# A hybrid Mamba-2 / Conformer step on one core: the chunk-state product of the scan as three float32r passes on split operands, instead of one plain float32 product

## The chip, the cores and the metric

The program runs on 1 core of one Trainium2 chip. The metric is the device time of one execution in microseconds (us), as the median of the timed runs.

## What is computed

Two decoder layers run over a prompt of 2048 tokens (width 1024) and 8 single-token samples. Layer 0 is a Mamba-2 SSD mixer, layer 1 a gated Conformer convolution. Inputs and outputs are float32. The change lies in the chunked scan of layer 0, over the prompt: 32 heads of 64 channels in 4 groups, state size 128, 16 chunks of 128 tokens. The reference, cut to that part:

```python
def ssd_scan(x, dt, A, Bm, Cm, h0, chunk):
    ...
    a_cum = jnp.cumsum(dts * A.reshape(G, R), axis=2)
    xdt = xs * dts[..., None]
    ...
    cb = jnp.einsum('bcqgn,bckgn->bcqkg', Cs, Bs)
    y_diag = jnp.einsum('bcqkg,bcqkgr,bckgrp->bcqgrp', cb, decay, xdt)
    states = jnp.einsum('bcqgn,bcqgr,bcqgrp->bcgrpn', Bs, jnp.exp(a_cum[:, :, -1:] - a_cum), xdt)
    chunk_decay = jnp.exp(a_cum[:, :, -1])
    def step(h, inp):
        dec, st = inp
        return dec[..., None, None] * h + st, h
    h_fin, prev = lax.scan(step, h_init, (chunk_decay, states))
    y_off = jnp.einsum('bcqgn,bcgrpn,bcqgr->bcqgrp', Cs, prev, jnp.exp(a_cum))
    y = y_diag + y_off
```

`states` is the product that the change touches: for one group and one chunk, B transposed (tokens x state, 128 x 128) against the weighted inputs of the group's 8 heads (128 tokens x 512 channels).

## The kernel before, in words

The large projections of the kernel (`mm_in`, line 163, and `out_mm`, line 709) are already made in three float32r passes: each operand is split into a rounded high part and the rest, and hi x hi, lo x hi and hi x lo are summed in PSUM. The small products of the scan are plain float32 matmuls.

The order of the work is written out by hand: each engine runs its instructions strictly in the order in which the code issues them, and tiles of a pool are given out in turn, so that a new tile waits until the last readers of the tile whose memory it takes are done. `bufs` is the number of such places.

The scan is a loop over 64 **units** `u`, one for each pair of group and chunk (16 chunks of a group one after the other). It is software-pipelined by one unit and woven with the projection of the gate z:

- `ssd_loads(u + 2)` brings xg (inputs), bcg (B and C) and rb (decay sums, one buffer) by DMA from the SP queue.
- `ssd_a(u + 1)` prepares a unit: the decay matrix E (eight heads, half started on ACT at L579, half on DVE at L581, exponentials on ACT at L589 and L591), eA on ACT (L586, L587), transposes of xg on TensorE into ps_tx (L595), the transpose of B and the product B x C into ps_b (L597, L598), then on DVE xdt (L601) and Xd (L602) out of ps_tx, bt on ACT (L604) out of ps_b, cbm on DVE (L606) and E times cbm on DVE (L609).
- `zstep` issues some steps of the z projection: 8 matmuls each, three steps for a z tile of 264, 256, 512, 512 and 512 columns in turn, 3 or 4 steps for a unit. Its results are copied out by ACT (zt, L525); the weights are split by ACT (wh, L98) and POOL (wl, L99).
- `ssd_b(u)` finishes a unit: eight heads' products on TensorE into ps_d (L621), the chunk's state product into ps_st (L623), the product with the carried state into ps_o (L636); then on DVE yt (L626, four times), yt's second part (L637), the state update (L638, L639) and the sum (L640), and a DMA of yt to DRAM issued by POOL (L641).

All PSUM tiles of the scan have one buffer. Xd, bt, yt, E, eA and xdt have two.

Of the kernel before, what the change touches and what calls it, by code (L numbers as in the profile page):

```python
# [7 lines left out]
F32 = mybir.dt.float32  # L8
F32R = mybir.dt.float32r
AF = mybir.ActivationFunctionType  # L10
ALU = mybir.AluOpType
# [4 lines left out]
P = 128  # L16
# [22 lines left out]
def hybrid_step(ctx: ExitStack, tc: tile.TileContext, I, O):  # L39
    nc = tc.nc  # L40
    V, A, G_, TE, SY = nc.vector, nc.scalar, nc.gpsimd, nc.tensor, nc.sync
# [476 lines left out]
    sd = Pool("ssd", 2)  # L518
# [24 lines left out]
    def zstep(n):  # L543
        for _ in range(n):
            next(zg, None)
# [7 lines left out]
    ld, stA, state = {}, {}, {}  # L553

    def ssd_loads(u):
        if u >= len(units):
            return
        g, c = units[u]
        j, cc = divmod(c, 4)
        xg = sd.tile([P, 4, P], "xg", bufs=3)  # L560
        SY.dma_start(xg, x_d[j][cc, :, 4 * g:4 * g + 4, :])
        bcg = sd.tile([P, 2, P], "bcg", bufs=3)
        SY.dma_start(bcg, bc_d[j][cc, :, g, :, :])
        rb = sd.tile([P, 8, P], "rb", bufs=1)
        SY.dma_start(rb, ac_d[c:c + 1, 8 * g:8 * g + 8, :].to_broadcast([P, 8, P]))
        ld[u] = (xg, bcg, rb)

    def ssd_a(u):
        if u >= len(units):
            return  # L570
        g, c = units[u]
        j, cc = divmod(c, 4)
        xg, bcg, rb = ld[u]
        hs = slice(8 * g, 8 * g + 8)
        E = sd.tile([P, 8, P], "E")
        for h in range(8):
            ah = acT[:, cc, j, 8 * g + h:8 * g + h + 1]
            if h < EA_:
                A.activation(E[:, h, :], rb[:, h, :], AF.Relu, bias=ah, scale=-1.0)  # L579
            else:  # L580
                V.tensor_scalar(E[:, h, :], rb[:, h, :], ah, 0.0, ALU.subtract, ALU.min)  # L581
        eA = None
        if c:
            eA = sd.tile([P, 4, P], "eA")
            rv = rb.rearrange("p (a two) t -> p a two t", two=2)
            A.activation(eA[0:64], rv[0:64, :, 0, :], AF.Exp)  # L586
            A.activation(eA[64:128], rv[64:128, :, 1, :], AF.Exp)  # L587
        if EA_:
            A.activation(E[:, :EA_], E[:, :EA_], AF.Exp, scale=-1.0)  # L589
        if EA_ < 8:  # L590
            A.activation(E[:, EA_:], E[:, EA_:], AF.Exp)  # L591
        px = pss.tile([P, 8, 64], "ps_tx")
        pxf = px.rearrange("p a b -> p (a b)")
        for i in range(4):
            TE.transpose(pxf[:, i * P:(i + 1) * P], xg[:, i, :], ident)  # L595
        pb = pss.tile([P, 2, P], "ps_b")
        TE.transpose(pb[:, 0, :], bcg[:, 0, :], ident)  # L597
        TE.matmul(pb[:, 1, :], bcg[:, 0, :], bcg[:, 1, :], start=True, stop=True)  # L598
        xdt = sd.tile([P, 8, 64], "xdt")
        Xd = sd.tile([P, 8, 64], "Xd")  # L600
        V.tensor_tensor(xdt, px, dtT[:, cc, j, hs].unsqueeze(2).to_broadcast([P, 8, 64]), ALU.mult)  # L601
        V.tensor_tensor(Xd, px, wtT[:, cc, j, hs].unsqueeze(2).to_broadcast([P, 8, 64]), ALU.mult)  # L602
        bt = sd.tile([P, P], "bt")
        A.activation(bt, pb[:, 0, :], AF.Copy)  # L604
        cbm = sd.tile([P, 1, P], "cbm", bufs=1)
        V.tensor_tensor(cbm[:, 0, :], pb[:, 1, :], tri, ALU.mult)  # L606
        if EM:
            G_.tensor_tensor(E[:, :EM], E[:, :EM], cbm.to_broadcast([P, EM, P]), ALU.mult)
        V.tensor_tensor(E[:, EM:], E[:, EM:], cbm.to_broadcast([P, 8 - EM, P]), ALU.mult)  # L609
        stA[u] = (E, eA, xdt, Xd, bt)  # L610

    def ssd_b(u):
        g, c = units[u]
        j, cc = divmod(c, 4)
        xg, bcg, rb = ld.pop(u)
        E, eA, xdt, Xd, bt = stA.pop(u)
        hs = slice(8 * g, 8 * g + 8)
        pd = pss.tile([P, 4, P], "ps_d")
        for h in range(8):
            o = 64 * (h % 2)  # L620
            TE.matmul(pd[o:o + 64, h // 2, :], xdt[:, h, :], E[:, h, :], start=True, stop=True)  # L621
        pst = pss.tile([P, 8, 64], "ps_st")
        TE.matmul(pst.rearrange("p a b -> p (a b)"), bt, Xd.rearrange("p a b -> p (a b)"), start=True, stop=True)  # L623
        yt = sd.tile([P, 4, P], "yt")
        for i in range(4):
            V.scalar_tensor_tensor(yt[:, i, :], xg[:, i, :], Dch[:, 4 * g + i:4 * g + i + 1], pd[:, i, :], ALU.mult, ALU.add)  # L626
        if c == 0:
            stt = sd.tile([P, 8, 64], "state", bufs=1)
            state[g] = stt
            V.tensor_copy(stt, pst)  # L630
        else:
            stt = state[g]
            po = pss.tile([P, 4, P], "ps_o")
            sf = stt.rearrange("p a b -> p (a b)")
            for i in range(4):
                TE.matmul(po[:, i, :], sf[:, i * P:(i + 1) * P], bcg[:, 1, :], start=True, stop=True)  # L636
            V.tensor_tensor(eA, po, eA, ALU.mult)  # L637
            (G_ if SP_ else V).tensor_tensor(stt, stt, dec[:, cc, j, hs].unsqueeze(2).to_broadcast([P, 8, 64]), ALU.mult)  # L638
            V.tensor_tensor(stt, pst, stt, ALU.add)  # L639
            V.tensor_tensor(yt, yt, eA, ALU.add)  # L640
        G_.dma_start(y_d[c][:, 4 * g:4 * g + 4, :], yt)  # L641
        if c == NC - 1:
            G_.dma_start(O["ssm_p"][:, g, :], stt.rearrange("p a b -> p (a b)"))
# [3 lines left out]
    ZLEAD = 9  # L647
    zstep(ZLEAD)
    ssd_a(0)
    done = ZLEAD  # L650
    for u in range(len(units)):
        ssd_a(u + 1)
        ssd_loads(u + 2)
        want = ZLEAD + (ZN - ZLEAD) * (u + 1) // len(units)
        zstep(want - done)
        done = want
        ssd_b(u)
# [298 lines left out]
    for i in range(NCH):  # L956
        hl, _, nt, _ = fr[i]
# [423 lines left out]
    for i in range(NCH):  # L1381
        hl, nt = fr.pop(i)[:2]
# [109 lines left out]
```

## Time and profile before

| | |
|---|---|
| median of 3 timed runs | 3116.99 us (3115.62 to 3121.19) |
| the profiled execution | 3112.42 us, span 3110.6 us |
| busy share of the span: TensorE (PE) / DVE / ACT / POOL | 97% / 76% / 50% / 43% |
| the scan's first and last state product (L623) | 622.7 us and 1164.2 us after the span's start |

PE is TensorE's matrix product and PEld its weight load, DVE is VectorE, ACT is ScalarE, POOL is GpSimd, SP is the engine that issues most DMAs. In the list of instruction groups, a row has line, engine, operation, output<-inputs, shapes and count, then the busy time in us and the mean of one in ns, and after the second bar the engine's idle time just ahead of them with what ended it. In the timeline, a row has start and duration in us, engine, line, operation and count; neighbouring instructions of one kind are one row, and a bracket gives the idle time ahead and its releaser. A busy PE is not PE at its peak, since matmuls overlap and their ends are modelled; so the distance between starts is used for what a group of matmuls takes. A plain float32 matmul of the code leaves two records on PE.

### The profile page before, as it was taken

To read this page: it belongs to the slowest core of one execution; us is meant where nothing else is said; L and a number is where in the kernel's file an instruction comes from. 1 tells how busy PE (TensorE), PEld (TensorE's weight loads), DVE (VectorE), ACT (ScalarE), POOL (GpSimd) and SP (SyncE) were. 2 spreads that over 40 slices of the span, in tenths; PEclk is the share of its full clock that TensorE was granted. 3 is DMA by queue.
4 is the path that set the end of the run, shared out by engine and by line. 5 is a ranking of instruction groups with operands and counts; after the bars stand their busy time and mean duration, and the time that the engine had idled before them with its cause. 6 is when DMAs were issued, how large, how long until landed. Compare 5 with 4: busy or idle time off the path is not lost. (4 is left out here: it accounts for less than half of the span.)

```text
span 3110.6 us, 43242 instructions
## 1 busy us (share of the span) xinstructions
PE 3016.1 (97%) x16379; PEld 2540.5 (82%) x16379; DVE 2354.4 (76%) x3200; ACT 1540.4 (50%) x2601; POOL 1325.5 (43%) x983
## 2 busy tenths in 40 slices
PE   7999999999999999999989999999999999899998
PEld 6788888878878787788878888888888888677776
DVE  6556777678888884555448999999999997667663
ACT  6444434445555544444445555555545544655553
POOL 2112333211111111323325777867867767355551
PEclk9999999999999999999999999999999999999999
DMA  4123444455555556444451221111112124533331
GB/s 153 59 81 128 133 132 134 136 169 184 170 186 173 187 157 222 159 154 163 163 174 43 60 68 52 58 54 52 58 61 62 49 68 150 179 125 125 133 128 56
DMA packets 258624, 373.12 MB, mean 120 GB/s; under 512 B 30136, under 2 KB 187032, under 8 KB 252272
## 3 DMA queue, kind: packets, MB, share of 16 engines
q1 hardware_dynamic: 129168, 280.62, 28.0%
q10 hardware_dynamic: 122656, 67.68, 7.3%
q0 software_dynamic: 6592, 22.05, 1.8%
q8 instruction: 129, 2.11, 0.3%
q14 instruction: 79, 0.65, 0.1%
HBM read 240.47 MB, written 129.82 MB: 119 GB/s over the span
## 5 line engine op out<-in xcount | busy, mean ns | idle before, releaser
L1041 DVE SCALAR_TENSOR_TENSOR ps_acc<-vt,cw,ps_acc 128x1024 f32<-128x1024 f32 x672 | 815.1, 1283 | 6.5 <-ACT ps_acc L1034 4.8
L1047 POOL TENSOR_TENSOR pacc<-pacc,pr 128x1024 f32<-128x1024 f32 x256 | 620.7, 2457 | 110.4 <-ACT pr L1046 107.7
L709 PE MATMUL ps_out<-wo_hi,hhi 128*128 128x512 f32 (+1 forms) x1088 | 433.9, 399 | 9.0 <-ACT hhi L714 9.0
L709 PE MATMUL ps_out<-wo_lo,hhi 128*128 128x512 f32 (+1 forms) x1088 | 426.9, 392 | 0.0
L163 PE MATMUL ps_h<-u_hi,wh 128*128 128x512 f32 (+2 forms) x1920 | 397.2, 349 | 14.6 <-ACT zt L1082 8.0
L709 PE MATMUL ps_out<-wo_hi,hlo 128*128 128x512 f32 x1024 | 401.7, 392 | 0.8 <-DVE hlo L720 0.8
L163 PE MATMUL ps_h<-u_lo,wh 128*128 128x512 f32 (+2 forms) x1920 | 393.0, 347 | 0.0
L163 PE MATMUL ps_h<-u_hi,wl 128*128 128x512 f32 (+2 forms) x1920 | 392.7, 347 | 0.3 <-POOL wl L99 0.3
L163 PEld LDWEIGHTS ps_h<-u_hi,wh 128*128 128x128 f32 x1920 | 316.4, 190 | 62.6 <-ACT zt L1082 9.1
L163 PEld LDWEIGHTS ps_h<-u_lo,wh 128*128 128x128 f32 x1920 | 315.8, 189 | 45.1
L163 PEld LDWEIGHTS ps_h<-u_hi,wl 128*128 128x128 f32 x1920 | 315.3, 189 | 45.4 <-POOL wl L99 0.5
L295 DVE SCALAR_TENSOR_TENSOR acc<-raw,cw,acc 128x512 f32<-128x512 f32 (+1 forms) x360 | 229.1, 645 | 131.8 <-ACT acc L287 71.7
L1046 ACT ACTIVATE pr<-vt,cw 128x1024 f32<-128x1024 f32 x256 | 287.9, 1147 | 72.9 <-POOL pacc L1047 53.5
L99 POOL TENSOR_TENSOR wl<-wraw,wh 128x1024 fp32r<-128x1024 f32 x86 | 214.2, 2491 | 192.2 <-ACT wh L98 189.3
L709 PEld LDWEIGHTS ps_out<-wo_hi,hhi 128*128 128x128 f32 (+1 forms) x1088 | 201.5, 185 | 55.1 <-ACT hhi L714 9.8
L709 PEld LDWEIGHTS ps_out<-wo_lo,hhi 128*128 128x128 f32 (+1 forms) x1088 | 201.1, 185 | 48.5
L709 PEld LDWEIGHTS ps_out<-wo_hi,hlo 128*128 128x128 f32 x1024 | 193.9, 189 | 39.4 <-DVE hlo L720 1.6
L641 POOL DMA_DIRECT2D y_d<-yt x64 | 38.8, 606 | 437.3 <-DVE yt L640 414.3
L163 PE MATMUL ps_mm<-u_hi,wh 128*128 128x512 f32 (+2 forms) x960 | 200.2, 351 | 3.4 <-ACT wh L98 3.4
L163 PE MATMUL ps_mm<-u_lo,wh 128*128 128x512 f32 (+2 forms) x960 | 197.7, 349 | 0.0
L163 PE MATMUL ps_mm<-u_hi,wl 128*128 128x512 f32 (+2 forms) x960 | 197.4, 348 | 0.0
L163 PEld LDWEIGHTS ps_mm<-u_hi,wh 128*128 128x128 f32 x960 | 158.9, 191 | 27.1 <-ACT wh L98 3.9
(308 smaller groups left out, 4892.1 us busy)
## 6 DMA issues: line engine op xcount, KB each, us to landing
rb<-ac_d SPq DMA_DIRECT2D x64, 512.0 KB, 4.3
z_d<-zt ACTq DMA_DIRECT2D x96, 256.0 KB, 2.9
wraw<-w_in SPq DMA_DIRECT2D x48, 512.0 KB, 3.3
xg<-x_d SPq DMA_DIRECT2D x64, 256.0 KB, 3.3
y_d<-yt POOLq DMA_DIRECT2D x64, 256.0 KB, 2.8
wraw_o<-w_out SPq DMA_DIRECT2D x32, 512.0 KB, 4.1
yl<-y_d SPq DMA_DIRECT2D x16, 1024.0 KB, 6.2
zl<-z_d SPq DMA_DIRECT2D x16, 1024.0 KB, 5.5
```

The lines of the kernel that those rows point to most:

```text
L99: (eng or G_).tensor_tensor(wl, raw, wh.bitcast(F32), ALU.subtract)
L163: TE.matmul(ps[:, :n], a[:, k, :], x[:, k, o:o + n], start=(j == 0 and k == 0), stop=(j == 2 and k == KD - 1))
L295: V.scalar_tensor_tensor(acc[:, :n], raw[:, k:k + n], cw[:, m, k:k + 1], acc[:, :n], ALU.mult, ALU.add)
L641: G_.dma_start(y_d[c][:, 4 * g:4 * g + 4, :], yt)
L709: TE.matmul(pos[nh][:m], a[q][:, r, :m], w[q][:, r, ns], start=(k == 0 and j == 0), stop=(k == MI - 1 and j == len(parts) - 1))
L1041: V.scalar_tensor_tensor(acc, vt[:, k:k + W], cw1[:, m, k:k + 1], acc, ALU.mult, ALU.add)
L1046: A.activation(pr, vt[:, kk:kk + W], AF.Copy, scale=cw1[:, m, kk:kk + 1])
L1047: G_.tensor_tensor(pacc, pacc, pr, ALU.add)
```

## The change

bt is kept as two float32r tiles, bth (rounded copy, ACT as before) and btl (the rest, a new DVE subtraction out of ps_b, L605). A new step `ssd_split(u)` splits Xd into Xdh (a copy on ACT, L619) and Xdl (a subtraction on POOL, L620); it is called in the loop ahead of `ssd_a(u + 1)`. The state product becomes three float32r matmuls that add up in ps_st: Xdh x bth, Xdh x btl, Xdl x bth (L636). Xd and yt go from two buffers to one; Xdh and Xdl have one each. Line numbers behind that place move: L606 is L607, L609 is L610, L621 is L632, L623 is L636, L626 is L639, L636 to L641 are L649 to L654.

```diff
-        Xd = sd.tile([P, 8, 64], "Xd")
+        Xd = sd.tile([P, 8, 64], "Xd", bufs=1)
...
-        bt = sd.tile([P, P], "bt")
-        A.activation(bt, pb[:, 0, :], AF.Copy)
+        bt = [sd.tile([P, P], f"bt{i}", F32R) for i in "hl"]
+        A.activation(bt[0], pb[:, 0, :], AF.Copy)
+        V.tensor_tensor(bt[1], pb[:, 0, :], bt[0].bitcast(F32), ALU.subtract)
...
+    xsp = {}
+
+    def ssd_split(u):
+
+        Xd = stA[u][3].rearrange("p a b -> p (a b)")
+        xsp[u] = [sd.tile([P, 512], f"Xd{i}", F32R, bufs=1) for i in "hl"]
+        A.activation(xsp[u][0], Xd, AF.Copy)
+        G_.tensor_tensor(xsp[u][1], Xd, xsp[u][0].bitcast(F32), ALU.subtract)
+
     def ssd_b(u):
...
+        Xs = xsp.pop(u)
...
         pst = pss.tile([P, 8, 64], "ps_st")
-        TE.matmul(pst.rearrange("p a b -> p (a b)"), bt, Xd.rearrange("p a b -> p (a b)"), start=True, stop=True)
-        yt = sd.tile([P, 4, P], "yt")
+        pstf = pst.rearrange("p a b -> p (a b)")
+        for i, (w_, x_) in enumerate(((bt[0], Xs[0]), (bt[1], Xs[0]), (bt[0], Xs[1]))):
+            TE.matmul(pstf, w_, x_, start=i == 0, stop=i == 2)
+        yt = sd.tile([P, 4, P], "yt", bufs=1)
...
     for u in range(len(units)):
+        ssd_split(u)
         ssd_a(u + 1)
```

DVE in the middle of the scan, one unit's `ssd_a` and the start of `ssd_b`; what stands in brackets is what the instruction waits for. Before:

```order
L601 TENSOR_TENSOR xdt<-ps_tx,dtT 128x512 [waits PE_49]
L602 TENSOR_TENSOR Xd<-ps_tx,wtT 128x512
L606 TENSOR_TENSOR cbm<-ps_b,tri 128x128 [waits Activation_49]
L609 TENSOR_TENSOR E<-E,cbm 128x1024 [waits DVE_49]
L626 SCALAR_TENSOR_TENSOR yt<-xg,Dch,ps_d 128x128 [waits DMAHW3_49,DMASW2_49,PE_49]
```

The same place in the changed kernel:

```order
L601 TENSOR_TENSOR xdt<-ps_tx,dtT 128x512 [waits PE_49]
L602 TENSOR_TENSOR Xd<-ps_tx,wtT 128x512 [waits Pool_49]
L605 TENSOR_TENSOR btl<-ps_b,bth 128x128 [waits Activation_49]
L607 TENSOR_TENSOR cbm<-ps_b,tri 128x128
L610 TENSOR_TENSOR E<-E,cbm 128x1024 [waits DVE_49]
L639 SCALAR_TENSOR_TENSOR yt<-xg,Dch,ps_d 128x128 [waits DMAHW3_49,DMASW3_49,PE_49]
```

The new subtraction btl stands ahead of cbm, and the write of Xd, which waited for nothing, now waits for POOL: its only place is read by POOL's subtraction for the unit before.

POOL's queue at the third to the sixth unit (y_d is the DMA of yt, wl the split of a z weight tile). Before:

```order
L99 TENSOR_TENSOR wl<-wraw,wh 128x1024 [waits DMAHW1_49,PE_49,Activation_49]
L641 DMA y_d_83<-yt 128x512 [waits DVE_49]
L641 DMA y_d_84<-yt 128x512 [waits DVE_49]
L641 DMA y_d_85<-yt 128x512 [waits DVE_49]
```

The same place in the changed kernel:

```order
L620 TENSOR_TENSOR Xdl<-Xd,Xdh 128x512 [waits PE_49,Activation_49]
L99 TENSOR_TENSOR wl<-wraw,wh 128x1024 [waits DMAHW1_49,Activation_49]
L654 DMA y_d_83<-yt 128x512 [waits DVE_49]
L620 TENSOR_TENSOR Xdl<-Xd,Xdh 128x512 [waits PE_49,Activation_49]
L654 DMA y_d_84<-yt 128x512 [waits DVE_49]
L620 TENSOR_TENSOR Xdl<-Xd,Xdh 128x512 [waits PE_49,Activation_49]
L654 DMA y_d_85<-yt 128x512 [waits DVE_49]
```

One subtraction now stands behind each DMA of yt: the Xdl of a unit is behind the yt of the unit before it.

## The prediction, made before the changed kernel was run

> **What bounds the kernel now.** I read the page first, then the windows of the scan, then the timeline of a few units. The page:
>
> ```profile
> span 3110.6 us, 43242 instructions
> ...
> PE 3016.1 (97%) x16379; PEld 2540.5 (82%) x16379; DVE 2354.4 (76%) x3200; ACT 1540.4 (50%) x2601; POOL 1325.5 (43%) x983
> ...
> ```
>
> PE looks like the bound, but that is an average. In the window of the scan (us, then busy time of PE, PEld, DVE, ACT, POOL, clock) and in the product's own rows:
>
> ```profile
> 612.00:1172.00 560.00, 549.41 (x3744) 449.21 (x3743) 457.68 (x1025) 285.96 (x652) 71.81 (x81) 0.99 0.56 176
> ...
> L623 PEld LDWEIGHTS ps_st<-Xd,bt x128: 186/188/189, 622.7 to 1164.2; 128*128 128x128 f32 x128
> ```
>
> From the first state product to the last it is 541.4 us for 63 unit distances, 8.59 us each (the last record, at 1164.2, is the second of a pair 0.1 us apart). PE, unit by unit:
>
> ```profile
> 830.24 1.09 PE L621 MATMUL ps_d<-E,xdt 128*64 128x128 f32 x16
> ...
> 839.45 1.09 PE L621 MATMUL ps_d<-E,xdt 128*64 128x128 f32 x16
> ...
> 846.09 1.09 PE L621 MATMUL ps_d<-E,xdt 128*64 128x128 f32 x16
> 847.11 1.12 PE L623 MATMUL ps_st<-Xd,bt 128*128 128x512 f32 x2
> 848.08 1.05 PE L636 MATMUL ps_o<-bcg,state 128*128 128x128 f32 x8
> ...
> 852.70 1.09 PE L621 MATMUL ps_d<-E,xdt 128*64 128x128 f32 x16
> 853.72 1.12 PE L623 MATMUL ps_st<-Xd,bt 128*128 128x512 f32 x2
> ...
> 858.50 2.11 PE L163 MATMUL ps_z<-u_hi,wh 128*128 128x512 f32 x8 [0.78 <-DVE zs L527]
> 860.45 1.98 PE L163 MATMUL ps_z<-u_lo,wh 128*128 128x512 f32 x8
> 862.26 1.97 PE L163 MATMUL ps_z<-u_hi,wl 128*128 128x512 f32 x8
> ```
>
> A unit with three 512-column z steps takes PE 9.21 us (830.24 to 839.45), one with three short steps 6.61 us (846.09 to 852.70); a long step is 1.82 us (1.81 between 860.45 and 862.26), which leaves 3.75 for the scan's own matmuls and 0.95 for a short step. The code gives the 63 units 198 steps (up to unit u, 9 + 201(u+1)/64 rounded down), in the order six short, nine long; walking them, PE's work adds up to 525 us, 16 us under the 541. Where the rest goes shows on DVE, here from one L640 to the next in a unit where PE is ahead:
>
> ```profile
> 853.46 0.68 DVE L640 TENSOR_TENSOR yt<-yt,eA 128x512 f32<-128x512 f32 x1
> 854.06 0.87 DVE L581 TENSOR_SCALAR E<-rb,acT 128x128 f32<-128x128 f32 x4
> 854.84 0.69 DVE L601 TENSOR_TENSOR xdt<-ps_tx,dtT 128x512 f32<-128x512 f32 x1
> 855.44 0.68 DVE L602 TENSOR_TENSOR Xd<-ps_tx,wtT 128x512 f32<-128x512 f32 x1
> 856.82 0.29 DVE L606 TENSOR_TENSOR cbm<-ps_b,tri 128x128 f32<-128x128 f32 x1 [0.69 <-ACT bt L604]
> 857.14 1.22 DVE L609 TENSOR_TENSOR E<-E,cbm 128x1024 f32<-128x1024 f32 x1
> ...
> 858.36 1.11 DVE L626 SCALAR_TENSOR_TENSOR yt<-xg,Dch,ps_d 128x128 f32<-128x128 f32 x4
> 859.39 0.69 DVE L637 TENSOR_TENSOR eA<-ps_o,eA 128x512 f32<-128x512 f32 x1
> 859.99 0.68 DVE L638 TENSOR_TENSOR state<-state,dec 128x512 f32<-128x512 f32 x1
> 860.71 0.69 DVE L639 TENSOR_TENSOR state<-ps_st,state 128x512 f32<-128x512 f32 x1
> 861.32 0.68 DVE L640 TENSOR_TENSOR yt<-yt,eA 128x512 f32<-128x512 f32 x1
> ```
>
> DVE's own round is 7.86 us (853.46 to 861.32) with one wait of 0.69. It is shorter than PE's mean (8.3) and PE's long units, longer than PE's short ones: in short units PE runs ahead and then waits. Two rivals stand close together, PE with 8.3 us and DVE with 7.86.
>
> **The change part by part.** *The product on PE.* Its slot today is 847.11 to 848.08, 0.97 us. A float32r pass of the same shape is 1.81/8 = 0.226 us (860.45 to 862.26); the first group, after other matmuls or a pause, was 0.14 longer (858.50 to 860.45 against 1.81). Three passes: 0.68 + 0.14 = 0.82, or 0.68 if nothing is lost at the seam. Gain 0.15 to 0.29; I take 0.16, since today's slot has such a start as well, 64 x 0.16 = 10 us of PE work. The Trainium skill ("FP8 and Floating Point Precision", TensorE Precision Notes) says that a true FP32 product takes four passes through the array. By that rule one pass of four goes, 0.226 us, and PE's sum would be 14 us instead of 10; the slot of 0.97 agrees with four passes of 0.226 and a start.
>
> *btl on DVE* (128x128 out of PSUM) is of cbm's kind: one place in DVE's queue, 0.32 us (856.82 to 857.14). It cannot hide in the wait for ACT's bt ahead of it, as it needs that bt itself.
>
> *Xdh on ACT* is a 128x512 copy:
>
> ```profile
> L525 ACT ACTIVATE zt<-ps_z 128x512 f32<-128x512 f32 x42 | 24.8, 590 | 11.0 <-PE ps_z L163 10.5 <-ACT zt L525 0.5
> ...
> ACT E L579 <- DMA rb<-ac_d: 133.6, 52, 4.2
> ```
>
> It is 0.59 us and stands ahead of L579, where ACT waits for rb 133.6/52 = 2.6 us each time. It needs Xd and, for its one buffer, the state product of the unit before, both long done. I cost it at nothing; without that cover it would be 0.6 us in L579 to bt, which today ends DVE's wait, so up to 0.6 a round.
>
> *Xdl on POOL, with one Xd buffer.* This is the term that decides. POOL's queue has the DMA of yt(u-1) ahead of Xdl(u); DVE's write of Xd(u+1) must wait until Xdl(u) has read Xd(u). So DVE's round now runs through POOL: L640 ends, POOL issues the DMA, POOL subtracts, and only then may DVE write Xd. Rows:
>
> ```profile
> 854.44 0.61 POOL L641 DMA_DIRECT2D y_d<-yt  x1 [2.17 <-DVE yt L640]
> ...
> 849.87 2.40 POOL L99 TENSOR_TENSOR wl<-wraw,wh 128x1024 fp32r<-128x1024 f32 x1 [3.82 <-ACT wh L98]
> ...
> L736 POOL TENSOR_TENSOR zl<-zl 128x1024 f32<-128x1024 f32 x16 | 42.5, 2656 | 75.5 <-ACT zl L805 75.5
> ...
> L736 POOL TENSOR_TENSOR zl<-zl 128x512 f32<-128x512 f32 x16 | 26.5, 1656 | 1.3
> ```
>
> L640 ends at 854.14, the issue starts 0.30 later and ends at 855.05. For Xdl the bounds are 1.20 (half of 2.40 for 128x1024) and 1.66 (128x512 in a chain of dependent steps); the chain's own difference between 1024 and 512 is 1.00, so I take 2.40 - 1.00 = 1.40. Xdl ends at 856.45, DVE starts Xd at about 856.50 instead of 855.44 and ends it at 857.18, past the point where bt lets it go today (856.82). Then btl and cbm, 0.64, and L609 starts at 857.82 instead of 857.14: 0.68 more. DVE's round becomes 8.54 us (8.34 to 8.80 with the two bounds).
>
> *The same POOL step on PE.* The third pass needs Xdl(u): L640(u-1) + 0.30 + 0.61 + 1.40 = 2.3 us after L640(u-1) ends. Where PE is ahead, as at 853.72, its third pass would start 0.14 + 2 x 0.226 later, at 854.3, and now has to wait until 854.14 + 2.3 = 856.4, some 2 us; but those are the units in which PE waits a little later today (0.78 at 858.50, for a copy in DVE's queue).
>
> *yt with one buffer.* L626 of a unit waits until the yt before has landed.
>
> ```profile
> DMA to landing us min/median/max: 2.3/2.8/5.1
> ```
>
> Issue at +0.30, landing at +3.1 after L640's end, and L626 comes at +4.2 (858.36 today) or later: free, save for the few at 5.1, which cost up to 1 us each. No other DMA moves; SP's queue keeps its order.
>
> *The sum.* Two ends for the 63 distances. If waits were fully evened out, the time would be the larger of PE's and DVE's sums; if nothing were evened out, each unit would take the larger of its own two. DVE's sum takes 2.0 off for the first unit of a group (no L637, L638, L640) and 0.17 on for what z puts into DVE's queue: L638's mean is 0.14 above the 0.68 of an undisturbed one, and the copies of z add some 0.03.
>
> ```profile
> L638 DVE TENSOR_TENSOR state<-state,dec 128x512 f32<-128x512 f32 x60 | 49.3, 822 | 0.0
> ```
>
> Walking the units, before: 525 and 551; the 541.4 of the trace lies 63% of the way. After, with 8.54 and PE 0.16 shorter: PE 515, DVE 543, unit by unit 563, and 63% of the way from 543 to 563 is 555.6: **14 us longer**. With 8.34 it is +6, with 8.80 +25. The profiled execution's 3112.4 (span 3110.6 and 1.8 around it) becomes 3126; the median of the runs shown, 3117, is 4.6 above that execution, and the forecast is 3131.
>
> **The rivals.** *PE stays the bound* (the other side): Xd is free before DVE gets there, and DVE's longer round fits into its waits. Then the 10 us of PE show: 3107. It decides from an Xdl that ends before 855.4, which is 0.35 us after the DMA's issue; no POOL row of 128x512 speaks for that. If POOL could run the subtraction while the DMA is issued it would come near. 0.12.
>
> *DVE's round grows by btl's 0.32 alone* (8.18), since POOL is quicker or bt is late anyway: the same sums give 520 and 552, so 540.4, -1 us: 3116, no change. 0.17.
>
> *More than the sum.* PE's waits also cost clock. In the scan, two stretches ran at half clock, one after waits of 0.81 and 0.79 us close together, one after 2.17:
>
> ```profile
> 647.15 0.63 PE L595 MATMUL ps_tx<-ident,xg 128*128 128x128 f32 x4 [0.81 <-DMA xg<-x_d]
> ...
> 649.11 3.22 PE L163 MATMUL ps_z<-u_hi,wh 128*128 128x512 f32 x8 [0.79 <-DVE zs L527]
> ...
> 683.68 1.88 PE L163 MATMUL ps_z<-u_hi,wh 128*128 128x256 f32 x8 [2.17 <-ACT zt L525]
> ...
> 649.80:653.22 3.42, 3.42 (x10) 2.64 (x9) 3.38 (x10) 1.86 (x5) 0.31 (x1) 0.50 0.50 144
> 683.93:687.35 3.42, 3.42 (x24) 2.91 (x23) 0.96 (x2) 1.33 (x2) 2.14 (x1) 0.50 0.53 164
> ```
>
> Each costs 3.42/2 = 1.7 us. z goes through its five tiles 13 times in the scan, each with a pair of short units in which PE can now wait 2 us: at most 13 x 1.7 = 22 us more, 3153. And POOL can hold up DVE: L638 took
>
> ```profile
> 850.92 1.89 DVE L638 TENSOR_TENSOR state<-state,dec 128x512 f32<-128x512 f32 x1
> ```
>
> beside POOL's split at 849.87, and 0.68 without. If Xdl fell on L609, L638 or L640 in every second unit, 32 x 1.2 = 38 us, 3155 with btl's part. The Trainium skill ("SBUF — State Buffer", "SBUF: two separate sides") has the rule: a DVE instruction with two SBUF inputs and a GpSimd one that reads SBUF block each other for the whole instruction. The trace agrees with it at 1.89. Against it here: Xdl starts 0.9 us after L640, when DVE is at xdt (one input in PSUM) and then waits. The clock has 0.08, the block 0.05.
>
> That the change doesn't do what it says would be ps_st still with float32 passes; the program has three products for each unit, so I give that nothing.
>
> **How the numbers follow.** The forecast has 0.58, its own range 3123 to 3142. About 0.2% (6 us) is what a measurement of this kernel can tell from no change: 3111 to 3123. Slower by more: the forecast but for 0.04 at its lower end, and the costly cases, 0.67; the same: 0.17 + 0.04 = 0.21; faster: 0.12. The range reaches from 3112, leaving out the faster case, to 3147, which leaves out most of the costly ones.
>
> **What would show it right or wrong.** ps_st on PE with 192 records, and about 0.8 us from its first start to ps_o's. Xdl at 1.2 to 1.66 us, starting 0.9 us after L640's end. Xd on DVE idle ahead with POOL Xdl as the releaser, about 1 us in most units; DVE's shortest round near 8.5 instead of 7.86, and hardly a wait left for bt. PE idle ahead of the third pass, released by POOL, in the short units. The forecast is wrong if the wait of Xd for POOL is short, if PE's sum falls by much more than 10 us, or if the time changes outside 610 to 1172 us.

## The result, and the profile after

| | before | after |
|---|---|---|
| median of 9 timed runs each, on one chip | 3116.99 us | 3134.03 us (3127.65 to 3146.5) |
| ratio, 95% interval | | 1.0057 [1.0042, 1.0071] |
| profiled execution / its span | 3112.42 / 3110.6 us | 3127.65 / 3125.8 us |
| scan, first to last state product | 541.4 us | 560.1 us |

The changed kernel is 17 us slower; 3131 was forecast. The profiled execution is the lowest of the nine. Its span is 15.2 us longer: the scan 18.7 longer, the rest 3.5 shorter.

The page of the changed kernel:

```profile
span 3125.8 us, 43620 instructions
...
PE 3015.1 (96%) x16443; PEld 2555.9 (82%) x16443; DVE 2447.8 (78%) x3264; ACT 1583.7 (51%) x2665; POOL 1405.4 (45%) x1047
```

The window of the scan (busy time of PE, PEld, DVE, ACT, POOL, then clock), and the state product by its middle pass, one record for each of the 64 units:

```profile
612.00:1172.00 560.00, 528.37 (x3679) 446.44 (x3678) 538.53 (x1065) 325.18 (x705) 150.25 (x141) 0.99 0.54 172
...
L636 PE MATMUL ps_st<-Xdh,btl x64: 392/397/402, 621.8 to 1181.9; 128*128 128x512 f32 x64
```

PE has 21 us less busy time in this window (549.41 before; the product's 10, and work that now lies behind the window's end) and DVE 81 more (457.68). btl is about 18 of those 81, and a longer L581 (below) is more than the rest; some of DVE's other work, too, now lies behind the window's end. POOL's 78 more are the subtractions, 1.3 us each.

The new product, in the timeline of PE:

```profile
873.49 0.50 PE L636 MATMUL ps_st<-Xdh,bth 128*128 128x512 f32 x1
873.83 0.39 PE L636 MATMUL ps_st<-Xdh,btl 128*128 128x512 f32 x1
874.06 0.40 PE L636 MATMUL ps_st<-Xdl,bth 128*128 128x512 f32 x1
874.30 0.94 PE L649 MATMUL ps_o<-bcg,state 128*128 128x128 f32 x7
```

From its start to ps_o's it is 0.81 us (873.49 to 874.30), where the plain float32 product took 0.97.

One round of DVE in a unit where PE is ahead, beside POOL:

```profile
857.26 0.68 DVE L653 TENSOR_TENSOR yt<-yt,eA 128x512 f32<-128x512 f32 x1
857.86 2.33 DVE L581 TENSOR_SCALAR E<-rb,acT 128x128 f32<-128x128 f32 x4
860.11 0.68 DVE L601 TENSOR_TENSOR xdt<-ps_tx,dtT 128x512 f32<-128x512 f32 x1
860.71 0.68 DVE L602 TENSOR_TENSOR Xd<-ps_tx,wtT 128x512 f32<-128x512 f32 x1
861.31 0.27 DVE L605 TENSOR_TENSOR btl<-ps_b,bth 128x128 fp32r<-128x128 f32 x1
861.51 0.27 DVE L607 TENSOR_TENSOR cbm<-ps_b,tri 128x128 f32<-128x128 f32 x1
861.82 1.22 DVE L610 TENSOR_TENSOR E<-E,cbm 128x1024 f32<-128x1024 f32 x1
...
865.99 0.68 DVE L653 TENSOR_TENSOR yt<-yt,eA 128x512 f32<-128x512 f32 x1
```

POOL at the same time:

```profile
858.24 0.56 POOL L654 DMA_DIRECT2D y_d<-yt  x1 [2.17 <-PE ps_st L636]
858.82 1.28 POOL L620 TENSOR_TENSOR Xdl<-Xd,Xdh 128x512 fp32r<-128x512 f32 x1
```

The round is 8.73 us (857.26 to 865.99) instead of 7.86, and no idle time stands in it. Both are units in which DVE also makes a small copy of z (L527, not in the rows shown); in units without it the undisturbed round is 0.05 to 0.07 shorter, 8.67 here and 7.79 in the kernel before. The forecast had Xd waiting for Xdl. Here the time sits inside L581: four instructions that took 0.87 together now take 2.33, and xdt starts at 860.11, when Xdl ends (858.82 + 1.28 = 860.10). In another unit, the third and fourth of the four as one row:

```profile
848.81 1.95 DVE L581 TENSOR_SCALAR E<-rb,acT 128x128 f32<-128x128 f32 x2
```

The first three are as short as before. The fourth starts at 849.01 and lasts 1.756, until POOL's subtraction (849.38, 1.29 long) is over. That it is so in nearly every unit is seen in the rows of L581, in the kernel before and in the changed one, and of Xdl (minimum, median and maximum in ns):

```profile
L581 DVE TENSOR_SCALAR E<-rb,acT x256: 276/282/358, 611.5 to 1151.6; 128x128 f32<-128x128 f32 x128
...
L581 DVE TENSOR_SCALAR E<-rb,acT x256: 272/281/1964, 610.0 to 1169.7; 128x128 f32<-128x128 f32 x128
...
L620 POOL TENSOR_TENSOR Xdl<-Xd,Xdh x64: 1272/1298/2338, 614.5 to 1178.8; 128x512 fp32r<-128x512 f32 x64
```

and in the group of L581 (busy us, mean ns), which was 55.7 and 283 in the kernel before:

```profile
L581 DVE TENSOR_SCALAR E<-rb,acT 128x128 f32<-128x128 f32 x252 | 142.6, 629 | 0.3 <-DMA rb<-ac_d 0.3
```

The median is unchanged and the mean has more than doubled: 60 of the 256 are held, about one in four (55 of them the fourth of a unit, five the first), by some 1.45 us on average, 87 us in all. DVE's main waits in the scan before (engine, tile and line, what it waited for, us in total, times, longest):

```profile
DVE cbm L606 <- ACT bt L604: 40.4, 57, 1.8
...
DVE eA L637 <- PE ps_o L636: 24.5, 33, 0.8
DVE yt L626 <- PE ps_d L621: 24.2, 23, 5.4
```

The waits in the changed kernel:

```profile
DVE Xd L602 <- POOL Xdl L620: 4.2, 3, 1.4
...
PEld ps_st L636 <- POOL Xdl L620: 28.1, 20, 2.4
...
PE ps_st L636 <- POOL Xdl L620: 19.8, 14, 2.0
...
ACT Xdh L619 <- PE ps_st L636: 34.6, 25, 3.3
...
DVE yt L639 <- PE ps_d L632: 9.6, 5, 3.8
...
DVE btl L605 <- ACT bth L604: 1.9, 2, 1.1
```

The buffer wait that the forecast rested on came three times. DVE now waits for PE and ACT hardly at all; it is the bound of most of the scan.

**Two theories.** *The hold* (the "port theory" of the expectations below): POOL's subtraction keeps DVE's L581 from ending, whatever the buffers are. *The buffer chain* (the "buffer theory", the forecast's): DVE is late because Xd has one place, which Xdl must have read; L581's length would then be an appearance. A third is PE's wait of 47.9 us for Xdl ahead of the third pass.

### The profile page after: what moved, and what is told of

Read it like the earlier page. It is cut to its first block, busy times and chain, and to the rows that moved or that the text cites. A ratio compares the mean times of both kernels' runs of the same rounds, so it can differ in the third digit from the quotient of the medians.

```text
span 3125.8 us, 43620 instructions
## 1 busy us (share of the span) xinstructions
PE 3015.1 (96%) x16443; PEld 2555.9 (82%) x16443; DVE 2447.8 (78%) x3264; ACT 1583.7 (51%) x2665; POOL 1405.4 (45%) x1047
## 5 line engine op out<-in xcount | busy, mean ns | idle before, releaser
L654 POOL DMA_DIRECT2D y_d<-yt x64 | 36.0, 563 | 379.9 <-DVE yt L653 332.9
```

## The experiments

### Everything but the subtraction

The low part Xdl is not made; the third pass takes Xdh again in its place.

```diff
-        xsp[u] = [sd.tile([P, 512], f"Xd{i}", F32R, bufs=1) for i in "hl"]
+        xsp[u] = [sd.tile([P, 512], "Xdh", F32R, bufs=1)] * 2
         A.activation(xsp[u][0], Xd, AF.Copy)
-        G_.tensor_tensor(xsp[u][1], Xd, xsp[u][0].bitcast(F32), ALU.subtract)
```

> The changed kernel without POOL's subtraction; the third pass takes Xdh a second time, so the low part of Xd is left out of the state product, and TensorE, ACT and btl do what they do in the changed kernel. If POOL's subtraction is what costs (by the port that it shares with DVE, or by Xd's one buffer): DVE's round falls from 8.7 to about 8.16 us, no wait ahead of the third pass, and the time comes back to 1 us under the kernel before (within 6 of it). If the rest of the change costs (btl, Xdh on ACT, yt's one buffer): at least 10 us over the kernel before.

The state product's middle pass and L581:

```profile
L635 PE MATMUL ps_st<-Xdh,btl x64: 390/397/402, 622.8 to 1158.2; 128*128 128x512 f32 x64
...
L581 DVE TENSOR_SCALAR E<-rb,acT x256: 275/278/370, 611.0 to 1145.8; 128x128 f32<-128x128 f32 x128
```

DVE's wait for bth, in the list of waits:

```profile
DVE btl L605 <- ACT bth L604: 42.4, 58, 1.7
```

Ratio to the kernel before 0.9967 [0.9948, 0.9987]; the scan is 535.4 us and DVE's round 7.98 (8.05 with the copy of z). So three passes, btl, Xdh and the single buffers of Xd and yt together are worth some 10 us (0.0033 x 3117; 4 to 16 by the interval, 6.0 in the profiled scan), more than the 1 us expected, and all of the loss hangs on the subtraction. The DMA of yt is still issued by POOL behind the same DVE instruction, and L581 takes 370 ns at most: it is the subtraction that holds, not the issue ahead of it. DVE has its wait for bth back.

### The subtraction alone, in the kernel before

Xd keeps its two buffers and the product stays plain float32. POOL subtracts xdt from Xd into a tile that nobody reads; ssd_split stands where it stands in the changed kernel, and yt has one buffer as there.

```diff
-        yt = sd.tile([P, 4, P], "yt")
+        yt = sd.tile([P, 4, P], "yt", bufs=1)
...
+    def ssd_split(u):
+        E, eA, xdt, Xd, bt = stA[u]
+        G_.tensor_tensor(sd.tile([P, 8, 64], "Xdl", bufs=1), Xd, xdt, ALU.subtract)
...
     for u in range(len(units)):
+        ssd_split(u)
         ssd_a(u + 1)
```

> The kernel before, its state product in float32 and Xd in two buffers as ever, with one more instruction: POOL subtracts two 128x512 tiles of the unit (Xd and xdt) at the place of Xdl in its queue, into a tile that nobody reads; yt has one buffer. Port theory: the fourth L581 of a unit lasts 1.7 instead of 0.28 us in most units, DVE's round is 8.4 to 8.7, and the time is 10 to 17 us over the kernel before. Buffer theory (the step as it was predicted), and a theory that TensorE's wait for the third pass costs: no change, within 4 us, since nothing waits for POOL here.

The state product (its weight loads) and L581:

```profile
L623 PEld LDWEIGHTS ps_st<-Xd,bt x128: 186/188/190, 622.3 to 1179.1; 128*128 128x128 f32 x128
...
L581 DVE TENSOR_SCALAR E<-rb,acT x256: 270/280/1958, 611.1 to 1166.7; 128x128 f32<-128x128 f32 x128
```

DVE in the middle of the scan, and then POOL:

```profile
856.61 2.33 DVE L581 TENSOR_SCALAR E<-rb,acT 128x128 f32<-128x128 f32 x4
858.86 0.68 DVE L601 TENSOR_TENSOR xdt<-ps_tx,dtT 128x512 f32<-128x512 f32 x1
```

```profile
857.57 1.28 POOL L647 TENSOR_TENSOR Xdl<-Xd,xdt 128x512 f32<-128x512 f32 x1
```

Ratio 1.0054 [1.0029, 1.0079]. One POOL instruction for each unit, with nobody waiting for its result and both places of Xd kept, costs as much as the whole change; the scan is 556.7 us, 15.3 longer, and DVE's round 8.48 (8.53 with the copy of z). 58 of the L581 are held, here until 858.85, when the subtraction ends. That speaks for the hold, against the buffer chain, and against PE's wait ahead of the third pass, which this kernel does not have.

### A second buffer for Xd

Two places for Xd in the changed kernel; the memory comes from zt.

```diff
-        Xd = sd.tile([P, 8, 64], "Xd", bufs=1)
+        Xd = sd.tile([P, 8, 64], "Xd")
...
-        zt = ztp.tile([P, 512], "zt")
+        zt = ztp.tile([P, 512], "zt", bufs=1)
```

> The changed kernel with two buffers for Xd again; the place comes from zt, which gets one buffer instead of two. Buffer theory: Xd no longer waits for Xdl, DVE's round falls by about 0.4 us or more and at least 8 us come back. Port theory: L581 is held as before, the time stays within 5 us of the changed kernel, some 17 us over the kernel before.

The same two rows:

```profile
L636 PE MATMUL ps_st<-Xdh,btl x64: 388/397/403, 626.1 to 1185.8; 128*128 128x512 f32 x64
...
L581 DVE TENSOR_SCALAR E<-rb,acT x256: 272/279/1959, 610.8 to 1173.6; 128x128 f32<-128x128 f32 x128
```

Ratio 1.0086 [1.0057, 1.0115], from four runs. The scan is 559.7 us where the changed kernel has 560.1, and the round 8.67 as there: the second buffer gives back nothing. The time as a whole is some 9 us above the changed kernel's (1.0086 against 1.0057, intervals that overlap), more than the 5 expected. The rest of this kernel's profiled span is 18 us longer than in the changed kernel (2584.1 against 2565.7). That is not zt's doing alone, since the profiled run of the experiment before this one, which leaves zt as it was, has 2587.1; why those executions are longer outside the scan is settled in part. Their mean granted clock is 0.988 and 0.987 where the changed kernel's is 0.990, and the stretches at half clock outside the scan cost 8 and 12 us more than there; the remaining 10 us or so stay open. Within the scan, where the kernels differ, the verdict does not hang on it.

### The subtraction on DVE

```diff
-        G_.tensor_tensor(xsp[u][1], Xd, xsp[u][0].bitcast(F32), ALU.subtract)
+        V.tensor_tensor(xsp[u][1], Xd, xsp[u][0].bitcast(F32), ALU.subtract)
```

> The changed kernel with Xdl subtracted on DVE instead of POOL, at the same place of the program (in DVE's queue behind yt's last sum, ahead of L581). Port theory: POOL no longer takes part, L581 back at 0.28 us; the 0.6 us of the subtraction fits into DVE's wait for bth, so that DVE's round stays at 8.0 us as in the kernel without the low part: scan 535 us, 6 to 10 us under the kernel before. If DVE's work as such decides (0.6 us more in each of 64 units, 39 us of DVE): round 8.6, scan 558 to 561, some 17 us over the kernel before.

The state product:

```profile
L636 PE MATMUL ps_st<-Xdh,btl x64: 390/397/402, 623.5 to 1157.6; 128*128 128x512 f32 x64
```

The subtraction and btl in the list of groups:

```profile
L620 DVE TENSOR_TENSOR Xdl<-Xd,Xdh 128x512 fp32r<-128x512 f32 x64 | 44.6, 696 | 0.0
...
L605 DVE TENSOR_TENSOR btl<-ps_b,bth 128x128 fp32r<-128x128 f32 x64 | 18.6, 291 | 9.6 <-ACT bth L604 4.7
```

Ratio 0.9972 [0.9955, 0.9989]: faster than the kernel before, with the scan at 534.1 us. DVE does 44.6 us more work and its round is 7.98, as without any subtraction: the 0.6 us fit into the wait for bth, which was 42.4 us without the subtraction and is down to 4.7. POOL's 1.3 us beside DVE cost more than DVE's own 0.7.

### The subtraction on POOL, but earlier

ssd_split(u + 1) is issued in ssd_b(u) behind TensorE's products, so that it stands ahead of the DMA of yt.

```diff
+        if u + 1 < len(units):
+            ssd_split(u + 1)
         yt = sd.tile([P, 4, P], "yt", bufs=1)
...
+    ssd_split(0)
     for u in range(len(units)):
-        ssd_split(u)
         ssd_a(u + 1)
```

> The changed kernel with the split of unit u+1 issued within the end of unit u, behind its matmuls and ahead of the DMA of yt in POOL's queue. Xdl no longer waits for DVE's L640 and runs while DVE is at L639 to L651. Port theory: the fourth L581 is back at 0.28 us, DVE's round about 8.2 us, no wait ahead of the third pass; 0 to 5 us under the kernel before, unless Xdl now falls on L610 or L651, both with two SBUF inputs (up to 1.2 us a unit where it does). If it is POOL's work as such, wherever it stands: still 10 us or more over the kernel before.

The state product and L581:

```profile
L636 PE MATMUL ps_st<-Xdh,btl x64: 392/397/402, 622.9 to 1164.8; 128*128 128x512 f32 x64
...
L581 DVE TENSOR_SCALAR E<-rb,acT x256: 271/278/1106, 611.1 to 1152.4; 128x128 f32<-128x128 f32 x128
```

The state's decay and the sum of yt in the list of groups:

```profile
L653 DVE TENSOR_TENSOR state<-state,dec 128x512 f32<-128x512 f32 x60 | 52.2, 870 | 0.0
...
L655 DVE TENSOR_TENSOR yt<-yt,eA 128x512 f32<-128x512 f32 x60 | 44.9, 748 | 0.0
```

One unit on DVE, and then POOL at the same time:

```profile
850.92 1.70 DVE L653 TENSOR_TENSOR state<-state,dec 128x512 f32<-128x512 f32 x1
852.66 0.69 DVE L654 TENSOR_TENSOR state<-ps_st,state 128x512 f32<-128x512 f32 x1
853.27 1.03 DVE L655 TENSOR_TENSOR yt<-yt,eA 128x512 f32<-128x512 f32 x1
```

```profile
849.68 2.40 POOL L99 TENSOR_TENSOR wl<-wraw,wh 128x1024 fp32r<-128x1024 f32 x1 [3.83 <-ACT wh L98]
852.04 1.72 POOL L620 TENSOR_TENSOR Xdl<-Xd,Xdh 128x512 fp32r<-128x512 f32 x1
```

Ratio 0.9999 [0.9981, 1.0017], scan 541.9 us. The loss is gone, the gain is not there. L581 is free again but for four, and undisturbed rounds are 7.98; now the subtraction meets L653 and L655, whose means are 870 and 748 ns against 816 and 680 in the kernel without it. Over 60 units that is 7.3 us, and the scan is 6.5 us longer than there. In the rows, L653 lasts 1.70, held by the split of a weight tile as it can be in the kernel before (1.89), and L655 1.03 beside Xdl, while L654 between them, which reads PSUM, keeps its 0.69. A place earlier moved the hold to other instructions.

### Earlier, with bth ahead of eA

As above, and TensorE's transposes and ACT's copy of bth are issued before eA's exponentials, which takes the wait for bth (39.4 us in the kernel above) out of DVE's round.

```diff
+        px = pss.tile([P, 8, 64], "ps_tx")
...
+        TE.matmul(pb[:, 1, :], bcg[:, 0, :], bcg[:, 1, :], start=True, stop=True)
+        bt = [sd.tile([P, P], f"bt{i}", F32R) for i in "hl"]
+        A.activation(bt[0], pb[:, 0, :], AF.Copy)
         eA = None
...
-        px = pss.tile([P, 8, 64], "ps_tx")
...
-        TE.matmul(pb[:, 1, :], bcg[:, 0, :], bcg[:, 1, :], start=True, stop=True)
...
-        bt = [sd.tile([P, P], f"bt{i}", F32R) for i in "hl"]
-        A.activation(bt[0], pb[:, 0, :], AF.Copy)
```

> The kernel with the early split (POOL's subtraction ahead of the DMA of yt), and ACT copies bth before it makes eA instead of after the exponentials. If DVE's round is what is left to gain: the wait for bth (39 us in 58 units) goes, the round falls from 7.98 to about 7.4 us (then the exponentials of ACT end last), and by the sum of the prediction (515 evened out, 534 unit by unit) the scan takes about 527 us: 12 to 16 us under the kernel before. If TensorE is the bound by now, no change against the early split alone (within 3 us).

The state product:

```profile
L636 PE MATMUL ps_st<-Xdh,btl x64: 393/397/402, 623.2 to 1158.0; 128*128 128x512 f32 x64
```

The state's decay, and the first step of yt with its wait, in the list of groups:

```profile
L653 DVE TENSOR_TENSOR state<-state,dec 128x512 f32<-128x512 f32 x60 | 56.5, 941 | 0.0
...
L641 DVE SCALAR_TENSOR_TENSOR yt<-xg,Dch,ps_d 128x128 f32<-128x128 f32 x256 | 71.7, 342 | 32.6 <-PE ps_d L632 29.8 <-issue 2.7
```

Ratio 0.9967 [0.9951, 0.9983], faster than the kernel before. The round came down as expected (7.3 to 7.7), the scan did not follow it (534.8 us where the sum gave 527): DVE now waits 29.8 us for PE's ps_d, where it was 14.8 in the kernel above, so PE sets more of the pace, and L653 is held more often (40 times instead of 29; 941 ns). The gain is about 10 us where 12 to 16 were expected, so the result lies between the two expectations.

### The kernel before, with bt ahead of eA

The same move in the kernel before: plain float32 product, no split.

```diff
+        px = pss.tile([P, 8, 64], "ps_tx")
...
+        bt = sd.tile([P, P], "bt")
+        A.activation(bt, pb[:, 0, :], AF.Copy)
         eA = None
```

> The kernel before with the same move alone: ACT copies bt before eA. The wait of cbm for bt (40 us in 57 units) goes, DVE's round falls from 7.86 to about 7.3 us; TensorE's sum stays at 525, unit by unit 538 to 540: scan about 534, 6 to 9 us under the kernel before. Against the run beside it this shows what the three passes are worth once DVE's round is short: 525 against 515, so 6 to 10 us.

The state product's weight loads, and the group of yt's first step:

```profile
L623 PEld LDWEIGHTS ps_st<-Xd,bt x128: 186/188/189, 623.0 to 1159.7; 128*128 128x128 f32 x128
```

```profile
L626 DVE SCALAR_TENSOR_TENSOR yt<-xg,Dch,ps_d 128x128 f32<-128x128 f32 x256 | 71.7, 342 | 35.9 <-PE ps_d L621 35.6
```

Ratio 0.9986 [0.9974, 0.9998], scan 536.6 us, round 7.37. The order alone is worth about 4 us (1 to 8), less than the 6 to 9 expected. Of the 10 us of the kernel above, then, some 6 would be left for the three passes; the two intervals overlap, so that share is an indication.

## Why the prediction was right, and where it was not

The time was right, by a chain that starts and ends at the right places and has one wrong link. The prediction named as a sign of being wrong that "the wait of Xd for POOL is short"; it was 4.2 us in all, so by its own sign the mechanism was wrong though the number held.

**PE's slot**: 0.82 forecast, 0.81 measured. The price read from the rows was right; a whole pass of 0.226 less would have been 0.74. The kernel without the subtraction is about 10 us faster (4 to 16) and its scan 6.0 shorter, which agrees with the 64 x 0.16 = 10 us of PE work; that no other part of the change gives time is not shown on its own.

**Xdl**: start 0.9 us after L640 forecast, 0.88 measured (858.82 against 857.94); duration 1.40 forecast, 1.29 measured. That lies about halfway between the lower bound, half of the 128x1024 row (1.20), and the price taken.

**The step that failed** is "DVE's write of Xd(u+1) must wait until Xdl(u) has read Xd(u)". The dependence exists, but it comes last in 3 units of 64, and a second buffer changes nothing. What delays DVE is the fourth L581, held until Xdl ends. Both mechanisms let DVE go on at the same event, the end of Xdl, which is why the number survived. The two differ in one thing: xdt stands behind the hold too. The forecast had Xd start 3.04 us after L640's start (856.50 less 853.46), it was 3.45 (860.71 less 857.26); against that the steps from Xd to L610 took 1.11 instead of 1.32. L610 starts 4.56 after L653's start where 4.36 was forecast; so the round is 8.73 and not 8.54. That the number held is luck in part: the two mechanisms happen to end at one event, and two errors go against each other. The buffer wait was to add 0.36 us to a round (the 0.68 forecast for L609, less btl's 0.32) and the hold adds 0.69, while btl adds 0.19 and not 0.32.

**The hold as a rival** had 0.05, with the reason that DVE would be at xdt by the time Xdl starts. By the records that was so: in the trace of before the four L581 end at 854.93 (854.06 + 0.87) and Xdl was put at 855.05, and without a hold the fourth one after the change would have ended at 849.29 (849.01 + 0.28), with Xdl's record at 849.38. A gap of 0.1 us was taken for safe, and only the instructions with two tensor inputs (L609, L638, L640) were considered.

**btl**: 0.32 forecast, 0.19 measured in the kernels without the hold (7.98 against 7.79, and 8.05 against 7.86 with the copy of z). The starts of btl and cbm are 0.20 apart here (861.31 to 861.51); cbm's 0.32, the price taken, holds L610's wait for cbm as well.

**Xdh** was costed at nothing, which holds, but not for the reason given: the state product of the unit before is not long done, ACT waits for it 34.6 us in 25 units. In the kernel without the subtraction it waits 67.0 us in 36 units, and that kernel is faster all the same: ACT's wait for rb is down from 133.6 us to 51.1 there, and DVE waits for bth hardly longer than for bt before (42.4 us against 40.4).

**PE's third pass** waits 2 us in short units, as forecast, 47.9 us in all. Nothing speaks for a cost of its own: the kernel with the subtraction alone has no such wait and an equal loss. In the changed kernel the subtraction costs more of the scan (535.4 to 560.1, 24.7 us, against 15.3), but it adds the same 0.69 us to DVE's round in both (7.98 to 8.67, 7.79 to 8.48), and the walk of the prediction gives about 27 and 17 us from the rounds alone.

**The sum** was sound where DVE bounds the scan. The forecast's 7.86 was a round with the copy of z, so the measured rounds with it are to be put in. The walk with 8.73 in place of 8.54 gives about 563 us; 560.1 was measured. With the 8.53 of the subtraction alone, PE unchanged, it gives about 558 (556.7 measured), with 8.05 some 536 (535.4 and 534.1). With rounds of 7.37 it falls short (527 for 534.8, 533.5 for 536.6). PE's waits for the copies of z (L525 and L527) do not shrink with DVE's round: 5.2 us before, 5.3 and 4.2 in these two; what else is missing from the sum is not worked out.

The clock took little: about 3 us more than before at half speed in the scan, from 13.7 us instead of 6.8.

## What to carry to other kernels

When work is moved to POOL, look at what DVE runs while POOL does, and a few tenths of a microsecond ahead of POOL's recorded start too: a DVE instruction that suddenly takes as long as POOL's, at an unchanged median, is the sign, and the list of waits does not show it, because it counts as busy. Before blaming a buffer for such a delay, add a buffer, and run the suspected instruction alone in the old kernel. A split of 128x512 was cheaper on DVE, in a wait that it had anyway, than "for nothing" on the idle POOL.

## What the runs showed of the hardware

A DVE TENSOR_SCALAR of 128x128 float32 with one tensor input took 1.76 us instead of 0.28 beside a POOL subtraction of two tensors in SBUF, and ended when that one ended. In the changed kernel 60 of the 256 L581 overlap Xdl in the records; these 60 are held, and no other. The Trainium skill ("SBUF — State Buffer", "SBUF: two separate sides") says that VectorE and GpSimd share a pair of ports under an exclusive lock, which a DVE instruction in a two-port mode also needs, not only one with two SBUF inputs, and that the first to start keeps it for its whole instruction. The end of the hold agrees with it; the start does not by the records, since the held L581 starts at 849.01, 0.37 us before the subtraction's record. No run here shows when POOL took the lock, that L581 runs in such a mode, or that it is a port that the two share.

DVE instructions with one input in PSUM were not held: L654 kept 0.69 us (852.66) beside Xdl at 852.04, and 47 of the 60 L652 of that kernel, which read ps_o, overlap Xdl and last 0.69 us at most. POOL's subtraction itself took 1.72 us in that row against the usual 1.3, so the delay can go both ways.
